# x brought by feature and by token, q's products ahead of v's, and eight expert pieces issued from ScalarE's queue, in a hybrid attention and mixture-of-experts block

## The chip, the core and the metric

The kernel runs on one core of a Trainium2 chip. The metric is the device time of one execution in microseconds (us); lower is better. TensorE (PE) multiplies, VectorE (DVE) and ScalarE (ACT) do elementwise work, GpSimd (POOL) does small work and some transfers, and SyncE (SP) issues most transfers. The DMA engines move data between the chip's memory (HBM) and the core's (SBUF). PSUM takes TensorE's results.

## What is computed

One layer over 512 tokens of 1024 features, all in float32:

```python
h = rmsnorm(x, norm_mix_g)
cb, cc, cu, q, k, v, f_logit, g_conv, g_att = split_cols(h @ w_in)
y_conv = (cb * causal_dwconv3(cc * cu)) @ w_conv_out
o = forgetting_attention(q, k, v, f_logit, b_forget)   # 16 heads of 64
m = sigmoid(g_conv) * y_conv + sigmoid(g_att) * (o @ w_att_out)
x = x + m @ w_out
x = x + hier_moe(rmsnorm(x, norm_ffn_g), ...)          # 32 experts, top 2 of the top group
return rmsnorm(x, norm_final_g)
```

The attention adds to each score the sum of `log_sigmoid(f_logit + b_forget)` between the key's token and the query's.

## The kernel before

**Precision.** An operand of most products is split into a high part (`hi`, a copy on ACT) and a low part (`lo`, a subtraction on DVE), and three products are summed: hi with hi, hi with lo, lo with hi (`mm3`). The expert weights are used as they come, without a split.

**Front (first 62 us).** `hT` holds the normalised x with features on the partitions, in eight blocks `k` of 128 features, hi and lo. Before, x comes by token in four blocks `xs[tb]` of 128 tokens and 1024 features. For each block ACT sums the squares (`square`), DVE makes the root by shifts and three refinement steps (`rsqrt_steps`), DVE, POOL or ACT scale the block by its factor and by `gmix`, PE transposes it eight times (`transp_x`), and ACT and DVE split the result into `hT` (`split_x`). Products for v (`v_mm`, 256 features of v and 16 forget logits) start as soon as a token block is in `hT`. After v come q's two pairs of heads and k's two (`qk_mm`, each 24 products of 512 columns). The forget logits `fz` go through `Abs`, `Exp` and a series on DVE to `acc`; PE transposes `acc` into `pf` between k's first and second pair; DVE scans `pf` and the sums `ncum` go out to HBM (`ncd`) and come back spread over the partitions (`nct`), one row for each head. The front stands in `tc.manual_schedule()`: on each engine its instructions keep the order in which they are written. Instructions from outside such a section (splits for the next heads' weights, transfers) may stand between them.

**Middle.** Attention over 16 heads (to about 240 us) is interleaved with the projections of the other heads. Then come the merges with `w_att_out` and `w_conv_out`, and the short convolution. The planner that orders these parts puts an instruction in its engine's queue where its operands are due; a queue is then worked off in order.

**The w_out stage.** `x2_block(c, tb)` computes 128 tokens by 256 features of `m @ w_out` in 24 products (`px`), DVE adds x, ACT takes the sum of squares. Two PSUM buffers take `px`. The first eight blocks are c = 0 and 1 over the four token blocks; each is followed by `x2_transp`, two transposes on PE and a copy on ACT. The router's weights `wr` come in five small transfers from POOL's queue, and DVE scales them by `gcol` (L727). The stage's last blocks and the routing stand in a hand-ordered section.

**Experts.** 192 pieces of 1 MB (`raw_g`, `raw_u`, `raw_d`) go through a ring of 18 buffers: eight in `wrawb`, which lies where `hT` and the operands of the merges were, two in `wraw` and five in `whl` (which hold `w_out`'s columns until the w_out stage is through with them), and three in `wrawx`. `prefetch(n)` issues the next n pieces on SP's queue. Every expert takes two pieces each of gate, up and down.

Of the kernel before, what the change touches and what calls it, by code (L numbers as in the profile page):

```python
# [24 lines left out]
P = 128  # L25
T = 512
# [18 lines left out]
def block_kernel(ctx, tc, x, norm_mix_g, w_in, w_v0f, conv_w, conv_b, b_forget, w_conv_out,  # L45
# [194 lines left out]
    NV = 4 * NK  # L240
    cols = const.tile([P, NV], F32, name="cols")
    ncd = dram.tile([NH, T], F32, name="ncd")
    with tc.tile_pool(name="s0", bufs=2) as s0:
        xs = [s0.tile([P, D], F32, name=f"xt{tb}", bufs=1) for tb in range(NTB)]
        gmix = s0.tile([P, D], F32, name="gmix", bufs=1)
        vrow = s0.tile([NV, P], F32, name="vrow", bufs=1)
        bfb = s0.tile([P, NH], F32, name="bfb", bufs=1)
        fz = s0.tile([P, NTB, NH], F32, name="fz", bufs=1)
        VW = CW + NH
        with tc.manual_schedule():  # L250
            nc.sync.dma_start(xs[0], x[0:P])
            nc.scalar.dma_start(gmix, norm_mix_g.rearrange("(o d) -> o d", o=1).to_broadcast([P, D]))

            sq0 = s0.tile([P, 1], F32, name="sq0", bufs=1)
            nc.scalar.activation(sq0, eps_t, AF.Square)
            raws, vw = [], ([], [])
            for i in range(2):
                raw = p_tile(f"raw_v{i}")[:, 0:HK * VW].rearrange("p (k f) -> p k f", k=HK)
                nc.sync.dma_start(raw, w_v0f[i].rearrange("p (k f) -> p k f", k=HK))
                raws.append(raw)  # L260
                if i == 0:
                    nc.sync.dma_start(xs[1], x[P:2 * P])
                for r, a in zip(vw, ("hi", "lo")):
                    r.append(pt_tile(a, i)[:, 0:HK * VW].rearrange("p (k f) -> p k f", k=HK))
            for tb in range(2, NTB):
                nc.sync.dma_start(xs[tb], x[tb * P:(tb + 1) * P])
            raws0 = {nm: load_raw(w_cols(c0), nm + "0") for nm, c0 in (("q", COL_Q), ("k", COL_K))}
            nc.scalar.dma_start(bfb, b_forget.rearrange("(o h) -> o h", o=1).to_broadcast([P, NH]))
            for i in range(3):
                nc.gpsimd.dma_start(vrow[i * NK:(i + 1) * NK], conv_w[i].rearrange("(k p) -> k p", p=P))  # L270
            nc.gpsimd.dma_start(vrow[3 * NK:4 * NK], conv_b.rearrange("(k p) -> k p", p=P))
            v_tiles(0)
            ss = [s0.tile([P, 1], F32, name=f"ss{tb}", bufs=1) for tb in range(NTB)]
            rstd = [s0.tile([P, 1], F32, name=f"rstd{tb}", bufs=1) for tb in range(NTB)]
            psv = {}

            def square(tb):
                sq = s0.tile([P, D], F32, tag="sq", name="sq", bufs=1)
                nc.scalar.activation(sq, xs[tb], AF.Square, accum_out=ss[tb])

            def factors(*tbs):
                return rsqrt_steps([(rstd[tb], ss[tb]) for tb in tbs], s0)

            pts = {}

            def scale_x(tb, h):
                hs = slice(h * T, (h + 1) * T)
                nc.vector.scalar_tensor_tensor(xs[tb][:, hs], xs[tb][:, hs], rstd[tb], gmix[:, hs],
                                               op0=ALU.mult, op1=ALU.mult)

            def transp_x(tb):
                for k4 in range(2):
                    pt = ps_t.tile([P, 4, P], F32, tag="t", name="pt")
                    for k in range(4):
                        kk = 4 * k4 + k
                        nc.tensor.transpose(pt[:, k], xs[tb][:, kk * P:(kk + 1) * P], identf)
                    pts[k4] = pt

            def split_x(tb, k4):
                ks, ts_ = slice(4 * k4, 4 * k4 + 4), slice(tb * P, (tb + 1) * P)  # L300
                nc.scalar.activation(hT[0][:, ks, ts_], pts[k4], AF.Copy)
                nc.vector.tensor_sub(hT[1][:, ks, ts_], pts[k4], hT[0][:, ks, ts_].bitcast(F32))

            def lo_v(i):
                for eng, ks in ((nc.vector, slice(0, 2)), (nc.gpsimd, slice(2, 4))):
                    eng.tensor_sub(vw[1][i][:, ks], raws[i][:, ks], vw[0][i][:, ks].bitcast(F32))

            def v_mm(tb, i):
                if i == 0:
                    psv[tb] = (psp if tb % 2 else ps_o).tile([P, 1, VW], F32, tag="proj" if tb % 2 else "o",  # L310
                                                             name=f"psv{tb}")
                for a, b in ((0, 0), (1, 0), (0, 1)):
                    for k in range(i * HK, (i + 1) * HK):
                        nc.tensor.matmul(psv[tb][:, 0], blk(hT[a], k, slice(tb * P, (tb + 1) * P)),
                                         blk(vw[b], k, slice(0, VW)),
                                         start=k == 0 and a == b, stop=k == NK - 1 and b == 1)

            def v_end(tb):
                v_out(0, tb, psv[tb])
                nc.vector.tensor_add(fz[:, tb], psv[tb][:, 0, CW:VW], bfb)  # L320
# [1143 lines left out]
```

## Time and profile before

| | |
|---|---|
| median of 3 runs | 1089.59 us (1088.72 to 1091.97) |
| the profiled execution's own time | 1089.54 us |
| its span, first to last instruction | 1087.9 us |
| mean granted TensorE clock | 0.989 of full speed |
| busy: PE, DVE, ACT, POOL | 97%, 55%, 34%, 4% of the span |
| data moved | 266.17 MB, mean 245 GB/s |
| share of the chain that ended last | PE 84%, DMA 10%, DVE 2%, ACT 2% |

The busy share of PE is no measure of how well it is used, since its matmuls are pipelined. What counts for a stage is which engine or transfer the others wait for there. All times in the text count from the first instruction of the span.

### The profile page before, as it was taken

Reading aid. Unit: us, or ns where it says so; the run is one execution under the profiler, and the core shown is the slowest. Engines: PE = TensorE matmul, PEld = TensorE weight load, DVE = VectorE, ACT = ScalarE, POOL = GpSimd, SP = SyncE. Lnnn points to the kernel's source line nnn. Section 1 sums busy time; section 2 is a strip of 40 time slices with the busy share of each in tenths; the row PEclk is TensorE's granted clock in tenths of the full one; section 3 lists DMA queues with packets and bytes.
Section 4 is the critical chain, followed back from the end, with each engine's and each line's share of the span. In section 5 each row is a group of like instructions: output and inputs, shape, how many; then the busy total and the mean of one; then the engine's idle time right before and its main releaser. Section 6 shows DMA issues by size and latency. Waiting matters only on the chain.

```text
span 1087.9 us, 13684 instructions
## 1 busy us (share of the span) xinstructions
PE 1050.1 (97%) x5281; PEld 680.6 (63%) x5281; DVE 596.2 (55%) x1197; ACT 367.5 (34%) x692; POOL 43.0 (4%) x54
## 2 busy tenths in 40 slices
PE   6999999999999999999989999999999999999993
PEld 4878787878888888888889533333333333433441
DVE  6687878674324444444433545555555555455555
ACT  3576767583223232233332222222222211122114
POOL 4000000000000000000100100000000000000001
PEclk8999999999999999999999999999999999999997
DMA  5321322213232323234495999999999999999992
GB/s 215 117 87 61 99 73 92 95 42 116 80 114 81 114 81 113 78 101 134 171 361 198 376 406 422 419 419 422 419 422 418 421 422 419 420 420 422 422 403 91
DMA packets 41893, 266.17 MB, mean 245 GB/s; under 512 B 5935, under 2 KB 5983, under 8 KB 11745
## 3 DMA queue, kind: packets, MB, share of 16 engines
q1 hardware_dynamic: 35712, 253.05, 58.6%
q10 hardware_dynamic: 3456, 7.61, 2.1%
q0 software_dynamic: 2656, 4.61, 1.2%
q8 instruction: 42, 0.69, 0.3%
q14 instruction: 27, 0.21, 0.1%
HBM read 265.01 MB, written 4.23 MB: 247 GB/s over the span
## 4 chain that ended last, share of the span: by engine, by line
PE 84%; DMA 10%; DVE 2%; ACT 2%; issue 1%; DVEq 0%; ACTq 0%; SPq 0%
PE pg L1069 17%; PE py L124 8%; PE py L1084 8%; PE pg L124 7%; DMA raw_u<-in_w_e_dram 6%; PE pk L1111 5%; PE px L124 4%; PE pu L124 4%; PE pc L124 4%; PE pb L124 4%; DMA raw_d<-in_w_e_dram 4%; PE psq L124 4%; PE psk L124 3%; PE psv L124 3%; PE o L520 2%; PE t L504 1%
## 5 line engine op out<-in xcount | busy, mean ns | idle before, releaser
L1069 PE MATMUL pg<-raw_u,XT 128*64 128x512 f32 x512 | 233.4, 598 | 3.6 <-DMA raw_u<-in_w_e_dram 3.6
L1069 PE MATMUL pg<-raw_g,XT 128*64 128x512 f32 x512 | 234.6, 599 | 0.0
L1112 DVE TENSOR_TENSOR m<-pk,m 128x512 f32<-128x512 f32 x240 | 149.0, 683 | 114.1 <-PE pk L1111 114.1
L1069 PEld LDWEIGHTS pg<-raw_g,XT 128*64 128x64 f32 x512 | 64.3, 136 | 94.4 <-issue 90.9
L1084 PE MATMUL py<-raw_d,hTe 128*64 128x512 f32 x512 | 116.9, 598 | 0.5 <-ACT hTe L1076 0.5
L1257 ACT ACTIVATE ta<-pg,rsl 64x512 f32<-64x512 f32 x32 | 21.9, 683 | 235.7 <-PE pg L1069 235.7
L1069 PEld LDWEIGHTS pg<-raw_u,XT 128*64 128x64 f32 x512 | 64.8, 136 | 32.9 <-issue 15.6
L1094 DVE TENSOR_TENSOR Y<-py,Y 64x512 fp32r<-64x512 f32 x62 | 42.7, 688 | 76.1 <-ACT Y L1093 76.1
L1093 ACT ACTIVATE Y<-py 64x512 fp32r<-64x512 f32 x62 | 36.6, 591 | 121.9 <-PE py L1084 98.7
L1084 PEld LDWEIGHTS py<-raw_d,hTe 128*64 128x64 f32 x512 | 34.0, 136 | 67.1 <-issue 59.7
L1111 PEld LDWEIGHTS pk<-Y,S 128*128 128x128 f32 x240 | 40.4, 188 | 53.8 <-issue 32.5
L1111 PE MATMUL pk<-Y,S 128*128 128x512 f32 x240 | 72.0, 422 | 0.0
L124 PE MATMUL pg<-hT_hi,whl_g 128*128 128x512 f32 x224 | 71.1, 390 | 0.0
L124 PE MATMUL px<-whl_o,mT_hi 128*128 128x256 f32 x256 | 48.4, 290 | 0.0
L124 PEld LDWEIGHTS pg<-hT_hi,whl_g 128*128 128x128 f32 x224 | 41.8, 188 | 8.4
L124 PE MATMUL psq<-hT_hi,whl_q 128*128 128x512 f32 x128 | 44.0, 404 | 0.0
L124 PE MATMUL pg<-hT_lo,whl_g 128*128 128x512 f32 x112 | 43.6, 389 | 0.0
L124 PE MATMUL psk<-hT_hi,whl_k 128*128 128x512 f32 x128 | 42.0, 398 | 0.0
L124 PE MATMUL py<-tT_hi,whl_y 128*128 128x512 f32 x128 | 40.7, 389 | 0.0
L124 PEld LDWEIGHTS px<-whl_o,mT_hi 128*128 128x128 f32 x256 | 40.2, 194 | 0.1
L124 PE MATMUL pb<-hT_hi,whl_b 128*128 128x512 f32 x128 | 40.0, 389 | 0.0
L124 PE MATMUL pc<-hT_hi,whl_c 128*128 128x512 f32 x128 | 40.0, 389 | 0.0
(291 smaller groups left out, 1908.8 us busy)
## 6 DMA issues: line engine op xcount, KB each, us to landing
raw_g<-in_w_e_dram SPq DMA_DIRECT2D x64, 1024.0 KB, 19.9
raw_u<-in_w_e_dram SPq DMA_DIRECT2D x64, 1024.0 KB, 20.4
raw_d<-in_w_e_dram SPq DMA_DIRECT2D x64, 1024.0 KB, 19.9
raw_g<-in_w_in_dram SPq DMA_DIRECT2D x7, 1024.0 KB, 4.8
raw_q<-in_w_in_dram SPq DMA_DIRECT2D x4, 1024.0 KB, 5.7
raw_k<-in_w_in_dram SPq DMA_DIRECT2D x4, 1024.0 KB, 6.6
nct<-ncd ACTq DMA_DIRECT2D x16, 256.0 KB, 3.1
raw_y<-in_w_att_out_dram SPq DMA_DIRECT2D x4, 1024.0 KB, 4.7
```

The costliest lines, as they stand in the source:

```text
L124: nc.tensor.matmul(ps, blk(lhs[a], k, lsl), blk(rhs[b], k, rsl), start=i == 0, stop=i == 3 * NK - 1)
L504: nc.tensor.transpose(ps[:, (qb - kb) * P:(qb - kb + 1) * P], Pt[:, P_OFF[qb] + kb * P:P_OFF[qb] + (kb + 1) * P], identf)
L520: nc.tensor.matmul(po[:, q0:], w, PT[b][:, PT_OFF[kb]:PT_OFF[kb] + n], start=kb == 0 and b == 0, stop=kb == NTB - 1 and b == 1)
L1069: nc.tensor.matmul(ps[r:r + DH], XT[:, k, j], w[k // 4][:, k % 4], start=k == 0, stop=k == NK - 1)
L1084: nc.tensor.matmul(py[n * DH:(n + 1) * DH], hTt[:, f], raws[f // 2][:, f % 2, n * T:(n + 1) * T], start=f == 0, stop=f == 3)
L1093: nc.scalar.activation(Y[hi, ns], py[hi], AF.Copy)
L1094: nc.vector.tensor_sub(Y[lo, ns], py[hi], Y[hi, ns].bitcast(F32))
L1111: nc.tensor.matmul(ps, S[:, tb * P:(tb + 1) * P], Y[:, ns], start=True, stop=True)
L1112: nc.vector.tensor_add(x2[:, tb, ns], ps, x2[:, tb, ns])
L1257: nc.scalar.activation(a, pg[0:DH], AF.Silu, scale=rsl[:, e:e + 1])
```

## The change

x arrives twice. By token (`xs`, two buffers for four blocks) it serves for the sums of squares alone: ACT sums blocks 0 and 2, DVE blocks 1 and 3. By feature (`x_t`, a transposed copy packed outside) it arrives as `xt`, in four pieces of 512 KB. All four factors are made at once (`Sqrt` on ACT, one refinement step on DVE). They are spread over the partitions by one float32 product of a matrix of ones with four diagonal blocks; ACT copies the result to `rb`. Then each feature block k is scaled on DVE (by `gmix`, now a column, and `rb`), copied to `hT` hi on ACT and subtracted to `hT` lo on DVE, and q's six products of that block follow it. v's products and k's come after. PE no longer transposes x, nor the convolution's columns `cols`, which come packed. `gmix` is issued from ACT's queue behind the two squares. k's pairs take the PSUM buffers `psp`, which q's took before; before the change they took `ps_o`. In the w_out stage the first eight expert pieces are written one behind each of the first eight blocks, on ACT's queue; before, they were written behind the loads of w_out's last two columns, on SP's queue. The rest of the ring stays on SP.

```diff
-            nc.sync.dma_start(xs[0], x[0:P])
-            nc.scalar.dma_start(gmix, norm_mix_g.rearrange("(o d) -> o d", o=1).to_broadcast([P, D]))
-            sq0 = s0.tile([P, 1], F32, name="sq0", bufs=1)
-            nc.scalar.activation(sq0, eps_t, AF.Square)
+            rawq = wraw.tile([P, NK, CW], F32, tag="wraw", name="raw_q0")
+            for tb in range(2):
+                nc.sync.dma_start(xs[tb], x[tb * P:(tb + 1) * P])
+            nc.sync.dma_start(rawq[:, 0:HK], wqd[:, 0:HK])
+            sq0 = s0.tile([P, 1], F32, name="sq0")
+            nc.scalar.activation(sq0, eps_t, AF.Sqrt)
+            for tb in range(NTB):
+                sq = s0.tile([P, D], BF, tag=f"sq{tb % 2}", name="sq")
+                if tb >= 2:
+                    xs.append(s0.tile([P, D], F32, tag="xs", name=f"xs{tb}", bufs=2))
+                    nc.sync.dma_start(xs[tb], x[tb * P:(tb + 1) * P])
+                if tb % 2 == 0:
+                    nc.scalar.activation(sq, xs[tb], AF.Square, scale=1.0 / 32, accum_out=ss[:, tb:tb + 1])
+                else:
+                    nc.vector.scalar_tensor_tensor(sq, xs[tb], 1.0 / D, xs[tb], op0=ALU.mult, op1=ALU.mult,
+                                                   accum_out=ss[:, tb:tb + 1])
+            for i in range(0, NK, 2):
+                nc.sync.dma_start(xt[:, i:i + 2], xsrc[:, i:i + 2])
+                if i == 2:
+                    nc.sync.dma_start(rawq[:, HK:], wqd[:, HK:])
+            nc.scalar.dma_start(gmix, norm_mix_g)
...
+            warm(ps_s.tile([P, T], F32, tag="s", name="pwarm0"), 30)
+            nc.scalar.activation(rt_, ss, AF.Sqrt, bias=eps_t)
+            nc.vector.tensor_scalar(vh, ss, EPS, -0.5, op0=ALU.add, op1=ALU.mult)
+            nc.vector.reciprocal(y, rt_)
+            nc.vector.tensor_mul(tn, y, y)
+            nc.vector.tensor_mul(tn, tn, vh)
+            nc.vector.scalar_tensor_tensor(rstd, tn, 1.5, y, op0=ALU.add, op1=ALU.mult)
+            for tb in range(NTB):
+                nc.vector.tensor_scalar_mul(dg[:, tb], identf, rstd[:, tb:tb + 1])
+            nc.tensor.matmul(pss, ones, dg.rearrange("p b t -> p (b t)"), start=True, stop=True)
+            split_q(0)
+            nc.scalar.activation(rb, pss, AF.Copy)
+            def feature(k):
+                nc.vector.scalar_tensor_tensor(xt[:, k], xt[:, k], gmix[:, k:k + 1], rb, op0=ALU.mult, op1=ALU.mult)
+                nc.scalar.activation(hT[0][:, k], xt[:, k], AF.Copy)
+            feature(0)
+            for k in range(NK):
+                if k + 1 < NK:
+                    feature(k + 1)
+                if k == 1:
+                    split_q(1)
+                nc.vector.tensor_sub(hT[1][:, k], xt[:, k], hT[0][:, k].bitcast(F32))
                 for a, b in ((0, 0), (1, 0), (0, 1)):
+                    for j in range(2):
+                        nc.tensor.matmul(psq[j], blk(wq[a], k, slice(j * P, (j + 1) * P)), hT[b][:, k],
                                          start=k == 0 and a == b, stop=k == NK - 1 and b == 1)
+            split_v(0)
+            split_v(1)
+            qk_out("q", 0, psq[0])
+            pv = v_mm(0)
+            wk = split_w(rawk, "k0")
+            for tb in range(1, NTB):
+                pn = v_mm(tb)
+                v_end(tb - 1, pv)
+                pv = pn
+                if tb == 1:
+                    qk_out("q", 1, psq[1])
+            v_end(3, pv)
...
             nc.scalar.activation(az, fz, AF.Abs)
             nc.scalar.activation(e, az, AF.Exp, scale=-1.0)
+            pk = qk_mm("k", 0, wk)
...
-        def prefetch(n):
+        def prefetch(n, eng=nc.sync):
...
-                nc.sync.dma_start(loaded[u], src)
+                eng.dma_start(loaded[u], src)
...
                 for tb in range(NTB):
                     block(o, tb)
+                    prefetch(1, nc.scalar)
                     if c > 0 or tb > 0:
                         x2_transp(c if tb > 0 else c - 1, (tb - 1) % NTB)
             o2 = load_o(2)
             o3 = load_o(3)
-            prefetch(NB_B)
```

## Rows read from the trace of the kernel before

**Rows 1.** Busy us by window: PE, PEld, DVE, ACT, POOL; granted clock, DMA share, GB/s.

```profile
580.00:600.00 20.00, 20.00 (x183) 19.43 (x182) 9.84 (x59) 3.97 (x14) 0.58 (x3) 1.00 0.55 205
640.00:660.00 20.00, 20.00 (x96) 8.02 (x96) 11.90 (x19) 4.65 (x8) 1.00 (x1) 1.00 1.01 419
```

**Rows 2.** Chain that ended last, merged, in order of time: start, us, what.

```profile
553.61 4.15 PE px L124 x24
557.98 2.81 PE px L124 x24
...
900.53 22.10 DMA raw_d<-in_w_e_dram
```

**Rows 3.** Issues on SP's queue: start, us, line, transfer.

```profile
537.70 0.42 SPq L704 DMA_DIRECT2D raw_g<-in_w_e_dram  x1
540.83 0.33 SPq L632 DMA_DIRECT2D m<-in_x_dram  x1
...
545.22 0.33 SPq L704 DMA_DIRECT2D raw_u<-in_w_e_dram  x1
...
590.53 0.33 SPq L704 DMA_DIRECT2D raw_u<-in_w_e_dram  x1
```

**Rows 4.** Timeline around 550 us, DVE and PE: start, us, idle before and releaser.

```profile
551.27 1.27 DVE L727 TENSOR_SCALAR wr<-wr,gcol 128x36 f32<-128x36 f32 x8 [5.46 <-DMA wr<-in_w_router_expert_dram]
552.98 0.63 PE L765 MATMUL pt<-identf,m 128*128 128x128 f32 x2 [3.47 <-issue]
```

**Rows 5.** Windows of 2 us: the columns of rows 1.

```profile
10.00:12.00 2.00, 0.66 (x5) 0.45 (x5) 2.00 (x3) 0.60 (x1) 1.76 (x2) 1.00 1.04 425
...
554.00:556.00 2.00, 2.00 (x12) 2.00 (x11) 1.55 (x3) 1.63 (x3) 0.00 (x0) 0.50 1.00 414
```

**Rows 6.** Transfers by line: queue, count, KB each, median us from issue to landing.

```profile
m<-in_x_dram SPq DMA_DIRECT2D x4, 512.0 KB, 3.5
wr<-in_w_router_expert_dram POOLq DMA_DIRECT2D x4, 32.0 KB, 7.4
gcol<-in_norm_ffn_g_dram POOLq DMA_DIRECT2D x1, 4.0 KB, 3.0
```

**Rows 7.** Timeline of the front: ACT, DVE and ACT's queue.

```profile
6.27 1.06 ACT L279 ACTIVATE sq<-xt 128x1024 f32<-128x1024 f32 x1 [3.38 <-DMA xt<-in_x_dram]
21.01 0.75 DVE L288 SCALAR_TENSOR_TENSOR xt<-xt,rstd,gmix 128x512 f32<-128x512 f32 x1
46.50 0.20 DVE L390 TENSOR_SCALAR f_e<-f_e 128x64 f32<-128x64 f32 x1
52.25 0.23 DVE L400 TENSOR_TENSOR f_acc<-f_acc,fz 128x64 f32<-128x64 f32 x1
66.35 0.33 ACTq L470 DMA_DIRECT2D nct<-ncd  x1
```

**Rows 8.** Chain that ended last, the first 65 us: start, us, what.

```profile
32.59 4.50 PE psv L314 x36
...
37.26 11.10 PE psq L124 x48
...
53.80 0.45 PE pf L404 x4
```

**Rows 9.** Groups by line, first 62 us: busy us, mean ns of one, idle before.

```profile
L302 DVE TENSOR_TENSOR hT_lo<-pt,hT_hi 128x512 fp32r<-128x512 f32 x8 | 5.2, 684 | 3.7 <-ACT hT_hi L301 3.6
L84 DVE TENSOR_TENSOR whl_k<-raw_k,whl_k 128x1024 fp32r<-128x1024 f32 x4 | 4.8, 1224 | 1.8 <-ACT whl_k L83 1.8
L301 ACT ACTIVATE hT_hi<-pt 128x512 fp32r<-128x512 f32 x8 | 4.6, 598 | 10.5 <-PE pt L296 10.5
L223 DVE SCALAR_TENSOR_TENSOR q<-psq,q 64x512 fp32r<-64x512 f32 x4 | 2.8, 689 | 1.4 <-ACT q L222 1.3
L189 DVE TENSOR_TENSOR v<-psv,v 128x128 fp32r<-128x128 f32 x8 | 2.3, 288 | 1.8 <-ACT v L188 1.8
L255 ACT ACT_TABLE_LOAD x1 | 1.3, 1283 | 1.4 <-PEq L1450 1.4
```

More of the change, by code (lines that the diff above doesn't have):

```diff
@@ L236, in proj_qk @@
                 yield
-    NV = 4 * NK
-    cols = const.tile([P, NV], F32, name="cols")
+    cols = const.tile([P, 4 * NK], F32, name="cols")
     ncd = dram.tile([NH, T], F32, name="ncd")
[L243 to L248, printed above, removed]
+    with tc.tile_pool(name="s0", bufs=1) as s0:
+        xt = s0.tile([P, NK, T], F32, name="xt")
+        gmix = s0.tile([P, NK], F32, name="gmix")
+        xs = [s0.tile([P, D], F32, tag="xs", name=f"xs{tb}", bufs=2) for tb in range(2)]
+        ones = s0.tile([P, P], F32, name="ones")
+        bfb = s0.tile([P, NH], F32, name="bfb")
+        fz = s0.tile([P, NTB, NH], F32, name="fz")
@@ L281, in factors @@
[L281 to L297, printed above, removed]
@@ new lines, in block_kernel, with split_q @@
+            v_tiles(0)
+            wq = ([], [])
+            for i in range(2):
+                for r, t in zip(wq, half(f"q0_{i}")):
+                    r.append(t.rearrange("p (k f) -> p k f", k=HK))
+            def split_q(i):
+                split(rawq[:, i * HK:(i + 1) * HK], wq[0][i], wq[1][i])
+            warm(ps_s.tile([P, T], F32, tag="s", name="pwarm0"), 30)
+            nc.scalar.activation(rt_, ss, AF.Sqrt, bias=eps_t)
+            nc.vector.tensor_scalar(vh, ss, EPS, -0.5, op0=ALU.add, op1=ALU.mult)
@@ L345, in block_kernel @@
-            f23 = factors(2, 3)
-            for h in range(2):
-                scale_x(1, h)
-                list(islice(f23, 1 + h))
-            v_mm(0, 1)
-            for tb in range(2, NTB):
-                nc.gpsimd.tensor_mul(xs[tb], xs[tb], gmix)
-            transp_x(1)
-            for k4 in range(2):
-                split_x(1, k4)
-                list(islice(f23, 2))
-            for _ in f23:
-                pass
-            nc.scalar.activation(xs[2][:, 0:T], xs[2][:, 0:T], AF.Copy, scale=rstd[2])
@@ new lines, in block_kernel, with v_mm @@
+            split_v(0)
+            split_v(1)
+            qk_out("q", 0, psq[0])
+            def v_mm(tb):
+                ps = (ps_s if tb % 2 else ps_o).tile([P, 1, VW], F32, tag="s" if tb % 2 else "o", name=f"psv{tb}")
+                for i in range(2):
+                    for a, b in ((0, 0), (1, 0), (0, 1)):
+                        for k in range(i * HK, (i + 1) * HK):
+                            nc.tensor.matmul(ps[:, 0], blk(hT[a], k, slice(tb * P, (tb + 1) * P)),
+                                             blk(vw[b], k, slice(0, VW)),
+                                             start=k == 0 and a == b, stop=k == NK - 1 and b == 1)
+                return ps
@@ new lines, in v_end @@
+            def v_end(tb, ps):
+                nc.vector.tensor_add(fz[:, tb], ps[:, 0, CW:VW], bfb)
+                v_out(0, tb, ps)
+            pv = v_mm(0)
[7 more added lines that the diff above has]
+            v_end(3, pv)
+            az, e, e2, sa, s2, acc = (s0.tile([P, NTB, NH], F32, name=f"f_{c}")
+                                      for c in ("az", "e", "e2", "s", "s2", "acc"))
```

121 lines of the change are left out of this document (27 added, 94 removed).

## The prediction, written before the change was run

> **What bounds the kernel now.** I read the windows first, from the end backwards. In the experts' part the DMA engines are busy all the time, at 419 GB/s [rows 1], and where PE has used up its lead the chain of waits is made of transfers: 22.10 us for one down piece [rows 2]. So the end is set by when this stream begins to run without a break, plus the bytes behind that moment. It begins late. Between 580 and 600 us the DMA engines are only 0.55 busy [rows 1]: the first eight pieces have long been issued, from 537.70 to 545.22, and the ring's next buffer that w_out's columns give back lets a piece go at 590.53 [rows 3]. Those buffers come free as PE works through the w_out stage. Hence two things follow. A us that PE gains anywhere before 590 us moves the stream, and so the end, by a us. And loading the first eight pieces earlier is worth nothing by itself: they are in place before the experts start either way, and the ring is full.
>
> Next I read what PE waits for ahead of 590 us. In the middle it is nearly always busy. Two places remain: the front, and one stall in the w_out stage. There DVE waits 5.46 us for the router's weights `wr` and scales them from 551.27 on; the sum of a block of `px` stands behind that in DVE's queue, PE has no third PSUM buffer, and it idles 3.47 us until 552.98 [rows 4]. Then the granted clock is 0.50, that is 1.2 GHz [rows 5], and the next 24 products take 4.15 us where the following 24 take 2.81 [rows 2]: 1.3 us more. The stall costs 4.8 us. Why is `wr` late? Its transfers are small (32 KB each) and take 7.4 us from issue to landing, while a small load at a quiet time took 3.0 [rows 6]; in these 4 us SP put seven pieces of 1 MB into the queues [rows 3].
>
> **The change, part by part: the pieces on ACT's queue.** Each piece is now written behind a block. ACT works its queue in order, and a block's square waits for DVE, so pieces behind squares leave one per block, about 3 us apart. Against this the planner may place pieces early. It does so on ACT: the sums `nct` for a later head go out at 66.35, before the scores of the heads ahead of it are through [rows 7]. On SP only one piece was placed ahead of the x load (537.70 against 540.83) although all eight lay in freed memory, and seven in a bunch behind it [rows 3]. I take ACT's pieces as spread, not one per block, so that two to four MB lie ahead of `wr` where eight did. The landing of `wr` then lies between 3.0 and 7.4 us [rows 6]. I take 5.9, 1.5 earlier than before. PE's stall shrinks from 3.47 to about 2.0. After idle stretches of that kind the clock stood at 1.00 (PE busy 0.66 of 2 us, [rows 5]), so I count the 1.3 us of slow products as saved too. The pieces cost ACT some 0.4 us each to issue [rows 3], eight times 3.2 us; ACT waits for most of this stage, but one issue can stand ahead of the last split of `mT` that PE needs: 0.3. Sum: -1.5 - 1.3 + 0.3 = **-2.5**. Bounds: -4.8 (no stall left) and +1.3 (a bunch as before, with `wr` a little later). The other pieces stay on SP; nothing there is moved past them but the last x load, which is now free of seven pieces behind it.
>
> **The front.** The anchor is `pf`, which ends at 53.80 + 0.45 = 54.25 [rows 8]: k's second pair and `nct` follow it in both kernels at the same distance. I build the new front up to there.
>
> - *Sums of squares.* A block of x took until 6.27 with `gmix` of the same size beside it [rows 7]; alone I take 5.0 for block 0 and 6.2 for block 1. ACT's square takes 1.06 [rows 7] and its sum 0.2; block 2 can only be issued then, at 6.3, and needs 3.5 [rows 6]: 9.8. DVE's square of block 1 is twice an instruction of 0.75 [rows 7]: 7.7, block 3 lands at 11.2, its square ends at 12.7.
> - *Factors.* Root on ACT, five tiny DVE steps of about 0.2 and four diagonal blocks (a 128x128 step took 0.29, [rows 9]): 15.1. The float32 product of 512 columns is not in the front; between one product of this width (0.23, 11.10/48, [rows 8]) and four of them, doubled by the clock (1.8), I take 0.6. ACT's copy 0.60 [rows 9]: 16.3.
> - *Eight feature blocks.* DVE does 0.75 [rows 7] and 0.68 [rows 9], with hops 1.5, so 12.0, and once 1.22 for the second half of q's low weights [rows 9]: 29.5. PE needs 11.1 for q's 48 products [rows 8] and runs behind DVE, even if its first products run at the lower clock. Two products are left after the last subtraction: 29.9.
> - *v and k.* 96 products of v at 4.50/36: 12.0; k's first pair 11.10/2 = 5.5 [rows 8]. PE is through at 47.4.
> - *Forget sums.* From 29.5 DVE has v's two low halves (about 1.3 each, from 1.22), q's four outputs at 0.69, k's two low halves at 1.22, v's eight outputs at 0.29 [rows 9]: 10.1, and many of them take turns with ACT. v's last block ends on PE at 41.9; I take its logits at 43.8. `Abs` and `Exp` are 0.3 each. `Exp` comes after `Sqrt` now, and a table load of 1.28 [rows 9] stands before it; before the change the front had one load, at 1.4 us, off the path. 45.7. The series ran from 46.50 to 52.48 with two splits of 1.22 inside [rows 7, 9]: 3.5 by itself, 45.7 + 3.5 = 49.2, and about half a split between: 49.8. PE waits for it from 47.4. `pf` ends at 50.3.
>
> So the front is worth 54.25 - 50.3 = **-4.0**. The transposes that PE no longer does and the refinement steps are all in this sum, since it was built afresh. Bounds: -6.4, if the sums come early and `pf` follows at 47.4; and -0.5, if `gmix`, issued behind ACT's second square at about 11, takes 7.4 as `wr` did among big loads (18.4 where 16.3 is needed), and the series a whole split more with the turns in full.
>
> The Trainium skill has a rule for the table load ("ScalarE: Activation LUTs", section "Table sets: the hidden batching unit"): exp and sqrt lie in different sets, and a switch costs about 2.66 us, since a drain of some 1.38 comes with the load. The trace has 1.28 for the load and shows no drain by itself. By the page `pf` would come 1.4 later, and the sum would be 1084.4.
>
> **Sum**, against the profiled execution's 1089.54 us (span 1087.9; the median of the runs is 1089.59): 1089.54 - 4.0 - 2.5 = 1083.0.
>
> **Rivals.**
>
> - *The pieces leave in a bunch.* For it: [rows 7], and seven in a bunch on SP. Then PE's stall stays: 1089.5 - 4.0 + 0.3 = 1085.8, 1084.5 to 1087.5.
> - *The front is lost.* `gmix` late by 2.1, the series late; PE idles between k's first pair and `pf` for five us or more, longer than the 3.47 that were followed by the lower clock [rows 4, 5], and pays 1.3 more. Front -0.5 + 1.3, stage -2.5 or 0: 1087.8 to 1090.3.
> - *Slower: a third queue starves `wr`.* With the eight pieces bunched on ACT, the x load on SP and `wr` on POOL, three queues share the engines. 8.4 MB at 419 GB/s [rows 1] are 20 us; if `wr` lands only when the pieces are through, at about 560 instead of 551.27, PE stalls 8.8 longer: 1089.5 - 4.0 + 8.8 = 1094. It decides from a landing at 558.5, which eats the front's 4.0 and 3.3 more. Against it: beside eight pieces on SP, `wr` landed after 7.4 [rows 6], long before they were through. The Trainium skill ("DMA: Bandwidth & Descriptors", section "Queues, rings and completion order") says that each engine takes turns among its queues by packet; by that a third queue takes a share from `wr` only while the x load lasts, about 1.3 us, and the time would be that of the bunch, near 1087.
>
> **Chances.** Forecast 0.50, bunch 0.28, front lost 0.14, slower 0.08. A measurement of this kernel tells a difference of about 0.3%, 3.3 us, from no change. Faster by more (below 1086.3): 0.46 of the forecast, 0.15 of the bunch, 0.03 of the third: 0.64. Slower by more (above 1092.8): 0.08, and 0.02 of the third: 0.10. Same: 0.26. Range: the two likeliest cases reach from 1078.3 (both bounds) to 1087.5, the third to 1090.3. I give 1078.5 to 1089.5, which leaves out most of the slower case and a part of the third. The likeliest one's own range is 1079 to 1086.
>
> **What would show it.** Right, if `pf` ends at about 50 us, q's products begin near 17 and DVE sets their pace, DVE's wait for `wr` is nearer to 4 us than to 5.5, no window after it shows the lower clock, and the piece now at 590.53 goes out some 6 us earlier, with the rest unchanged. Wrong, if the pieces follow each other on ACT's queue within 4 us, if `gmix` ends DVE's wait before the first feature block, or if PE idles longer than 4 us ahead of `pf`; and altogether if the end does not move with the piece of 590.53.

## The result, and the profile after

| | before | after |
|---|---|---|
| median, runs side by side | 1089.15 us (4 runs) | 1100.30 us (4 runs, 1098.80 to 1101.89) |
| the profiled execution, its span | 1089.54, 1087.9 | 1098.80, 1097.1 |
| mean granted TensorE clock | 0.989 | 0.983 |

The change is slower: the ratio is 1.0101, with a 95% interval of 1.0080 to 1.0122, so 11 us, where 6.5 us less were forecast. The end did move with the stream: the piece that went out at 590.53 [rows 3] goes out at 599.59 now, 9.06 later, and the span is 9.2 longer. So the loss lies ahead of that point. The attention's read-out begins 3.2 us later (257.8 against 254.6, the first of the 128 `py` products of `oT_hi`), and the w_out stage adds another 5.9.

Timeline of the front after the change, rows of SP, DVE, PE and ACT: start, us, engine, line, instruction, idle time before it and what ended it.

```profile
6.06 1.62 SPq L265 DMA_DIRECT2D xs<-in_x_dram  x2
...
12.95 1.22 DVE L269 SCALAR_TENSOR_TENSOR sq<-xs 128x1024 bf16<-128x1024 f32 x1 [5.48 <-DMA xs<-in_x_dram]
...
19.08 1.41 DVE L320 SCALAR_TENSOR_TENSOR xt<-xt,gmix,dg 128x512 f32<-128x512 f32 x2 [1.67 <-ACT dg L315]
...
23.52 1.22 DVE L84 TENSOR_TENSOR whl_q<-raw_q,whl_q 128x1024 fp32r<-128x1024 f32 x1 [1.64 <-ACT whl_q L83]
...
30.99 1.47 DVE L329 TENSOR_TENSOR hT_lo<-xt,hT_hi 128x512 fp32r<-128x512 f32 x2
...
16.34 2.08 PE L313 MATMUL pss<-dg,ones 128*128 128x512 f32 x2 [6.81 <-DVE dg L312]
20.55 2.07 PE L332 MATMUL psq<-hT_hi,whl_q 128*128 128x512 f32 x4 [2.13 <-ACT hT_hi L321]
...
25.41 0.73 PE L332 MATMUL psq<-hT_lo,whl_q 128*128 128x512 f32 x2 [0.23 <-DVE hT_lo L329]
...
34.16 0.67 PE L348 MATMUL psv<-PThi,hT_hi 128*128 128x272 f32 x4
...
55.94 1.01 PE L385 MATMUL pf<-identf,f_acc 128*16 128x128 f32 x4 [4.07 <-DVE f_acc L382]
...
50.23 0.25 ACT L369 ACTIVATE f_az<-fz 128x64 f32<-128x64 f32 x1
50.50 1.28 ACT L370 ACT_TABLE_LOAD   x1
51.79 0.26 ACT L370 ACTIVATE f_e<-f_az 128x64 f32<-128x64 f32 x1
```

The last block of x lands at 12.95, the float32 product that spreads the factors takes 2.08 after 6.81 us of idle, and the first feature block starts at 19.08. At 25.41 PE waits for the low half of the second block. That subtraction stood in DVE's queue behind the second half of q's low weights (23.52), for which DVE had waited 1.64 for ACT's copy. PE then still has 38 of q's 48 products to do, 8.75 us up to v's first product at 34.16, while DVE is through with its last subtraction at 32.46. `Abs` stands at 50.23, 4.0 us behind v's last product. PE then waits 4.07 us for the series, and `pf` ends at 56.95 where it ended at 54.25 [rows 8]. What follows is slow as well. The chain that ended last, first of the kernel after, then of the same front with the old ring (start, us, what):

```profile
55.94 1.01 PE pf L385 x4
56.95 6.59 PE psk L124 x24
```

```profile
56.06 1.01 PE pf L385 x4
57.07 7.85 PE psk L124 x24
```

24 such products take half of 11.10, 5.55 [rows 8]; here 6.59 and 7.85. The windows of the kernel after (columns as in [rows 1]) show the lower clock at the start and behind the idle stretch:

```profile
0.00:20.00 20.00, 10.37 (x32) 3.73 (x32) 6.63 (x20) 5.76 (x10) 3.43 (x12) 0.87 0.82 283
20.00:40.00 20.00, 19.23 (x95) 16.21 (x96) 16.83 (x22) 12.42 (x17) 0.00 (x0) 0.87 0.36 142
...
50.00:60.00 10.00, 5.93 (x23) 4.38 (x22) 5.41 (x18) 3.53 (x7) 1.35 (x3) 0.83 0.02 5
...
550.00:560.00 10.00, 7.87 (x59) 7.70 (x58) 1.93 (x10) 1.56 (x6) 0.00 (x0) 0.88 0.77 237
...
570.00:580.00 10.00, 7.38 (x46) 6.74 (x46) 5.48 (x6) 5.17 (x9) 0.00 (x0) 0.83 0.84 310
```

The w_out stage after the change, same view, rows of ACT and its queue, DVE and PE:

```profile
540.91 0.34 ACTq L684 DMA_DIRECT2D raw_g<-in_w_e_dram  x1
542.37 0.34 ACTq L684 DMA_DIRECT2D raw_u<-in_w_e_dram  x1
549.26 0.33 ACTq L684 DMA_DIRECT2D raw_g<-in_w_e_dram  x1
...
571.66 0.34 ACTq L684 DMA_DIRECT2D raw_u<-in_w_e_dram  x1
572.32 3.89 ACT L83 ACTIVATE whl_o<-raw_o 128x1024 fp32r<-128x1024 f32 x4
...
547.81 0.17 DVE L726 TENSOR_SCALAR vs<-vi 128x4 int32<-128x4 int32 x1 [4.09 <-POOL vi L724]
...
555.50 1.28 DVE L707 TENSOR_SCALAR wr<-wr,gcol 128x36 f32<-128x36 f32 x8 [6.44 <-DMA wr<-in_w_router_expert_dram]
...
548.78 0.44 PE L745 MATMUL pt<-identf,m 128*128 128x128 f32 x2 [2.31 <-DVE m L738]
557.20 0.41 PE L745 MATMUL pt<-identf,m 128*128 128x128 f32 x2 [2.13 <-issue]
571.66 0.41 PE L745 MATMUL pt<-identf,m 128*128 128x128 f32 x2 [0.39 <-DVE m L738]
573.42 0.39 PE L124 MATMUL px<-whl_o,mT_hi 128*128 128x256 f32 x1 [1.35 <-ACT whl_o L83]
574.68 0.58 PE L124 MATMUL px<-whl_o,mT_hi 128*128 128x256 f32 x1 [0.87 <-DVE whl_o L84]
```

The pieces do leave spread out, 540.91 to 571.66, two of them ahead of x's load. But there are two stalls of PE ahead of 560 instead of one of 3.47 [rows 4], and a third place at 571 to 575 that did not exist (0.39, 1.35 and 0.87): the four splits of w_out's last two columns, on ACT and then on DVE, stand behind all eight pieces. Before, DVE had them at 538.98, 554.45, 555.93 and 566.58, between the blocks. DVE's small steps on the tokens' numbers (`vs`) moved as well: before, they stood behind the first sum of `px`; now they are ahead of it, and wait 4.09 for POOL. PE's waits in the stage add up to 7.05 us, against 3.47; that is 3.6 of the 5.9. The products between them are slower as well: the granted clock is 0.83 from 570 to 580.

### The profile page after: what moved, and what is told of

It is laid out like the page before. It is cut to its first block, busy times and chain, and to the rows that moved or that the text cites. A ratio compares the mean times of both kernels' runs of the same rounds, so it can differ in the third digit from the quotient of the medians.

```text
span 1097.1 us, 13606 instructions
## 1 busy us (share of the span) xinstructions
PE 1051.5 (96%) x5260; PEld 681.0 (62%) x5260; DVE 593.5 (54%) x1173; ACT 366.0 (33%) x689; POOL 33.1 (3%) x48
## 4 chain that ended last, share of the span: by engine, by line
PE 74%; DMA 18%; DVE 4%; ACT 2%; issue 1%; POOL 0%; SPq 0%; DVEq 0%; ACTq 0%
PE pg L1050 13%; DMA raw_u<-in_w_e_dram 11%; PE py L124 8%; PE pg L124 7%; PE py L1065 6%; DMA raw_d<-in_w_e_dram 5%; PE pu L124 4%; PE pc L124 4%; PE pb L124 4%; PE px L124 4%; PE pk L1092 4%; PE psk L124 3%; PE psv L124 3%; PE psq L124 3%; PE o L500 2%; PE t L484 1%
## 5 line engine op out<-in xcount | busy, mean ns | idle before, releaser
L124 PE MATMUL pu<-hT_hi,whl_u 128*128 128x512 f32 x128 | 40.0, 389 | 0.0
```

The lines of the kernel that those rows point to most:

```text
L124: nc.tensor.matmul(ps, blk(lhs[a], k, lsl), blk(rhs[b], k, rsl), start=i == 0, stop=i == 3 * NK - 1)
```

## The experiments

Ratios are to the kernel before, timed beside each; the medians of before were 1089.05 to 1089.50. Where the intervals of two runs overlap, the difference between them is not shown.

| run | median us | ratio, 95% interval |
|---|---|---|
| e1 front alone | 1094.77 | 1.0047 (1.0031 to 1.0062) |
| e2 ring alone | 1094.62 | 1.0049 (1.0036 to 1.0062) |
| e3 ring in its new places, SP's queue | 1093.90 | 1.0040 (1.0027 to 1.0054) |
| e4 before without DVE's two waits | 1084.47 | 0.9953 (0.9940 to 0.9966) |
| e8 e4 and ring on ACT's queue | 1089.53 | 1.0001 (0.9993 to 1.0010) |
| e9 ring on POOL's queue behind wr | 1087.72 | 0.9984 (0.9975 to 0.9993) |
| e12 e8, splits early | 1091.78 | 1.0017 (1.0006 to 1.0028) |
| e13 e12, first four pieces on SP | 1084.47 | 0.9957 (0.9943 to 0.9971) |
| e5 e1, 62 warm products | 1094.63 | 1.0048 (1.0034 to 1.0062) |
| e6 e1, `pf` behind k's second pair | 1094.04 | 1.0042 (1.0029 to 1.0055) |
| e7 e1, Exp's table early | 1092.73 | 1.0033 (1.0023 to 1.0043) |
| e10 e1, forget chain early | 1089.28 | 0.9997 (0.9988 to 1.0006) |
| e14 e10, four blocks of x at once | 1085.82 | 0.9966 (0.9955 to 0.9976) |
| e11 e10 and e4's stage | 1084.23 | 0.9953 (0.9940 to 0.9967) |
| e15 e14 and e4's stage | 1082.47 | 0.9938 (0.9925 to 0.9951) |

### The two halves of the change

**e1**, the front with the old ring:

```diff
-                    prefetch(1, nc.scalar)
...
             o3 = load_o(3)
+            prefetch(NB_B)
```

> The changed kernel with the ring as it was: the eight pieces again behind the loads of w_out's columns on SP's queue. My theory says that the two halves of the change add: the front costs +3.3 us (the read-out products py start at 257.99 in the changed kernel, 254.72 before), the w_out stage +5.8. So this kernel should be 3.3 us slower than the one before, near 1092.5, with the w_out stage (start of py 254.7 +3.3; wr's wait 5.5, PE's stall 3.5; four splits of o2 and o3 between 553 and 567 less their shift) as before. The rival, that the front is good for its predicted -4.0 once the ring does not disturb it, expects 1085.1; a third, that the front's own late end is hidden further on, expects 1089.2.

5.3 us slower. The stage is as before (one stall of 3.65). The front is dearer than the 3.2 us read off the kernel after, because the 24 products behind `pf` took 7.85 here and 6.59 there; up to that point the two executions differ by 0.1 us.

**e2**, the ring's edit in the kernel before:

> The kernel before with nothing but the ring's edit: one piece behind each of the first eight blocks, on ACT's queue. My theory: the stage costs +5.8 us by itself, so about 1095, with three things in the trace: DVE waits about 4 us for POOL's iota ahead of the first sums of px, PE stalls about 2 us for them, and the four splits of o2 and o3 stand behind all eight pieces at about 569, with PE waiting for them. The rival says that this order is a result of the new front (a different start of the stage in the plan) and that the ring alone gives the predicted -2.5, near 1087.

5.2 us slower, with the stalls of the kernel after (2.28, 1.27, 0.39, 1.35 and 0.88). The halves add: 5.3 + 5.2 = 10.5 of 11.

**e3**, the changed kernel with `prefetch(1)` where it has `prefetch(1, nc.scalar)`:

> The changed kernel with the pieces written in the same places, behind the blocks, but issued from SP's queue. If what costs 5.8 us is that the pieces are work of ACT in the plan, which then moves the splits behind them and the steps on the tokens' numbers ahead of the sums, this kernel has the order of before on ACT and DVE and is near 1092.5, like the one with the front alone. If what costs is the place (pieces issued later, in turn with the blocks) or the load on the DMA engines, it stays near 1098 to 1100.

4.4 us slower, the same as the front alone within the intervals; one stall of 3.73, the splits between the blocks. So the place in the program costs nothing; the queue, with what follows from it, does.

### What the stage's price is made of

**e4**, `gcol` into ACT's copies of the transposed x2, and POOL's `iota` moved ahead of the `wr` transfers:

```diff
-            for k in range(NK):
-                nc.vector.tensor_scalar_mul(wr[:, k, 0:36], wr[:, k, 0:36], gcol[:, k:k + 1])
...
-                nc.scalar.activation(x2T[c][:, :, tb * P:(tb + 1) * P], pt, AF.Copy)
+                for k in range(2):
+                    nc.scalar.activation(x2T[c][:, k, tb * P:(tb + 1) * P], pt[:, k], AF.Copy,
+                                         scale=gcol[:, 2 * c + k:2 * c + k + 1])
```

> The kernel before, with DVE's wait for the router's weights taken away: gcol multiplies the transposed x2 where ACT copies it, not wr, and POOL makes the tokens' numbers ahead of the wr transfers. This asks for the price that my prediction put on the stall alone: 3.5 us of PE idle and 1.3 of slow products, so -4.8, near 1084.7, with the piece that goes out at 590.53 leaving at about 585.7. The rival: PE's stall is only moved (to the splits of w_out's last columns, or to ACT, which gets 16 more short copies), and the time stays within 1 us of before.

5.0 us faster; PE has no stall in the stage, and the ring's piece leaves at 585.30, where 585.7 was expected (issue on SP's queue: start, us, line, transfer):

```profile
585.30 0.33 SPq L704 DMA_DIRECT2D raw_u<-in_w_e_dram  x1
```

So the price that the prediction put on the stall, 4.8, was right.

**e9**, `prefetch(NB_B, nc.gpsimd)` in the kernel before: the pieces on POOL's queue, seven of eight behind `wr`.

> The kernel before, with the eight pieces on POOL's queue, seven of them behind the five transfers of the router's weights wr, so that only one piece and w_out's columns are ahead of or beside wr; ACT's and DVE's orders stay, but for the small steps on the tokens' numbers. My prediction held that the pieces make wr late (7.4 us from issue to landing): by it wr lands after 3 to 5 us here, DVE's wait falls from 5.5 to 2 or 3 us, and the time falls by 2 to 4.8, to 1084.5 to 1087. The rival, which the runs so far speak for (7.2 to 8.7 us whether the pieces are bunched or spread), says that wr is slow by itself, since it is made of packets of 16 and 32 bytes: it lands after about 7, the stall stays at 3.5, and the time at 1089.

Transfers by line (queue, count, KB each, median us from issue to landing), DVE's wait in e9 and PE's stall there:

```profile
wr<-in_w_router_expert_dram POOLq DMA_DIRECT2D x4, 32.0 KB, 6.8
```

```profile
549.64 1.28 DVE L727 TENSOR_SCALAR wr<-wr,gcol 128x36 f32<-128x36 f32 x8 [4.87 <-DMA wr<-in_w_router_expert_dram]
...
551.35 0.41 PE L765 MATMUL pt<-identf,m 128*128 128x128 f32 x2 [2.23 <-issue]
```

6.8 us with one piece ahead, 7.4 with eight beside it [rows 6], as medians of four transfers. What DVE waits for is the last of them. That wait ends at 549.64 and not at 551.27, 1.6 earlier (1.2 if counted from the first issue of `wr`), and PE's stall is 2.23 and not 3.47. So the pieces account for 1.2 to 1.6 us of `wr`'s lateness, and the rest is its own. The time falls by 1.8.

**e8**, e4 with the ring on ACT's queue:

> The kernel before with the ring's edit and without DVE's two waits (gcol taken into ACT's copies of the transposed x2, POOL's tokens' numbers ahead of the wr transfers), to be set beside the same kernel with the old ring, which took 1084.5. What is left of the ring's price is then what the late splits of o2 and o3 cost. My theory says about 4 us, 1088.5: the four splits still stand behind the eight pieces and PE waits for them at about 569. The rival: the price was the two waits, and this kernel takes 1084 to 1085.

5.1 us above e4. The four splits stood behind the pieces, and PE waited 1.59 and 0.88 for them, as expected; a wait of 0.39 just ahead was for the last sum. That this is the whole price was put to the test in **e12**: the loads of the last two columns written earlier.

```diff
                     block(o, tb)
+                    if c == 0 and tb == 2:
+                        o2 = load_o(2)
+                    if c == 1 and tb == 2:
+                        o3 = load_o(3)
                     prefetch(1, nc.scalar)
...
-            o2 = load_o(2)
-            o3 = load_o(3)
```

> The kernel before with the ring on ACT's queue and without DVE's two waits, as in the run that took 1089.5, and with the loads of w_out's last two columns written earlier, behind the third block of each of the first two columns, so that their splits stand between the pieces and not behind all eight. If the late splits are the rest of the ring's price, the time falls by about 5 us to that of the same kernel with the old ring, 1084.5, and PE no longer waits at 565. The rival: the pieces themselves cost it (issues among ACT's squares and copies, a third queue), and the time stays at 1088.5 to 1089.5.

My theory fell: the splits stood between the blocks, and the time did not fall; it rose by 2.3 in the medians (1.7 by the ratios, whose intervals touch). The timeline of e12, DVE and PE, names another wait:

```profile
553.65 0.42 DVE L756 TENSOR_TENSOR m<-px,m 128x256 f32<-128x256 f32 x1 [5.98 <-DMA m<-in_x_dram]
...
554.18 0.66 PE L763 MATMUL pt<-identf,m 128*128 128x128 f32 x2 [3.72 <-DVE m L756]
556.18 0.80 PE L124 MATMUL px<-whl_o,mT_hi 128*128 128x256 f32 x2 [1.34 <-ACT whl_o L83]
```

The fourth block's sum needs x's last load, and that is late. From issue to landing it took 8.0 us before (the row in [rows 6] is the median of four x loads and hides it), 8.2, 7.8 and 8.9 in e1, e3 and e4, and 11.9 and 11.7 in e2 and e8. The transfer rows of e2:

```profile
m<-in_x_dram SPq DMA_DIRECT2D x1, 512.0 KB, 11.9
wr<-in_w_router_expert_dram POOLq DMA_DIRECT2D x4, 32.0 KB, 8.7
```

**e13**, e12 with the first four pieces on SP's queue and the last four on ACT's:

```diff
-                    prefetch(1, nc.scalar)
+                    prefetch(1, nc.scalar if c > 0 else nc.sync)
```

> The last kernel (ring behind the blocks, no waits of DVE, splits of w_out's last columns early, 1091.8), with the first four pieces on SP's queue, behind which x's last load stands as before, and only the last four on ACT's. Theory: what costs now is x's last load. It shares the DMA engines with pieces on ACT's queue, lands 11.7 to 12 us after its issue where it took 8.0 to 8.9 in kernels without pieces there, and the sum of the fourth block waits for it (5.98 us in the last kernel, PE 3.7). So here x lands after 8 to 9, that wait is gone, and the time is that of the old ring without DVE's waits, 1084.5 (to 1085.5). Rival: pieces issued from ACT cost by themselves, or the order of the splits does: 1088 or more.

1084.47, the time of e4 to the hundredth, with four pieces still issued from ACT; PE has no stall, and x lands after 7.9 (that the medians agree to the hundredth is chance; within the intervals they are the same):

```profile
m<-in_x_dram SPq DMA_DIRECT2D x1, 512.0 KB, 7.9
```

In e8 the same late x cost PE 0.59 only, and the splits 2.47 with a clock of 0.86 around them; in e12 it is the other way round. In e2, and in the kernel after, the late x cost nothing, since DVE was still waiting for `wr` when x had landed (552.25 and 552.74 in e2). Which wait counts depends on the order; both come with the first pieces on ACT's queue. So neither ACT's issues nor pieces behind squares were seen to cost anything. What costs is the first pieces on ACT's queue, and what they reorder. e13 also gave ACT and DVE nearly the order of before, so it does not part x's load from the order by itself; that the load matters with the splits in place is e12's row.

Why x is late is not settled. In the kernel after, e2, e8 and e12 two pieces, 2 MB, go out ahead of x's load (in e2 at 537.51 and 538.97, x at 540.35). In all other runs one does (before: 537.70, x at 540.83). At the 415 GB/s of the kernel before, 1 MB more takes 2.5 us, by estimate, and x is 2.8 to 3.9 later. e9 speaks for this second reading: its pieces were on POOL's queue beside SP's, one ahead of x, and x landed after 8.7. Two pieces on SP's own queue ahead of x would decide it, and were not tried. The same doubt holds for `wr`, which is late too in these runs, 8.4 to 9.1 against 6.8 to 7.5 in the others.

### The front

**e5**, 62 warm products instead of 30:

> The front alone (changed kernel, ring as before), with 62 warm products at the start where there were 30, so that PE is busy until the float32 product that spreads the factors. In the front alone PE idled 6.8 us ahead of that product, which took 2.08 us and was followed by a clock of 0.86 over the first 40 us. My theory puts about 1 us of the front's loss on that product and 1 to 2 on q's first products at the lower clock: pf ends 1 to 2.5 us earlier than its 57.1 there, time about 1092.5 against 1094.8. Rival: DVE sets the pace of the eight feature blocks, PE catches up in any case, and only the product's own us is won or nothing.

Nothing (1094.63 against e1's 1094.77). The float32 product took 1.12 instead of 2.08, and DVE's first block began at 18.29, 0.9 earlier than in e1. But PE idled 2.14 and 2.28 between q's products, and those behind the second idle were slow, four in 1.70 where four take 1.07 later on. PE in e5:

```profile
24.63 0.72 PE L332 MATMUL psq<-hT_lo,whl_q 128*128 128x512 f32 x2 [2.28 <-DVE hT_lo L329]
25.19 1.70 PE L332 MATMUL psq<-hT_hi,whl_q 128*128 128x512 f32 x4
...
34.99 0.67 PE L348 MATMUL psv<-PThi,hT_hi 128*128 128x272 f32 x4
```

v's first product came at 34.99, later than the 34.26 of e1, and `pf` at 56.77, not 56.06; only the 24 products behind `pf` were quicker, 6.33 against 7.85. So PE waits for DVE up to the second block's low half, and from there on its own products set q's end. That is neither the prediction's reading, in which DVE sets the pace to the end, nor this run's theory.

**e6**, `pf` behind k's second pair:

```diff
             pk = qk_mm("k", 0, wk)
+            pk1 = qk_mm("k", 1, wk)
...
-            qk_out("k", 1, qk_mm("k", 1, wk))
+            qk_out("k", 1, pk1)
```

> The front alone, with pf's four transposes written behind k's second pair, so that PE does not wait for the forget series between the pairs. My theory: the 4.1 us of idle ahead of pf and the slow products behind it (5 to 11 of them, 1 to 2.5 us) are the price of the late series; without them k's second pair ends near 57.4, against 64.8, and the time falls by 5 to 6 us to about 1089. Rival: the sums nct come some 1.5 us later by this and the first scores have to wait for them, so that most of it is lost again: 1092 to 1094.

0.7 us won, not 5, and even that lies within the intervals. PE's idle is gone and comes back behind it: 2.57 and 0.97 for k's outputs, which now stand behind the scan, and the first use of `nct` waits until 65.70. The rival was right about the loss; it is shared between k's outputs and `nct`.

**e7**, one `Exp` of a single column on ACT behind v's splits:

> The front alone, with one Exp of a single column on ACT ahead of q's outputs, so that the table of Exp is loaded there (ACT has time then) and not between Abs and Exp. The load of 1.28 us leaves the forget chain: pf earlier by 1.3, and by up to 2.7 if the Trainium skill's figure for a switch (page ScalarE: Activation LUTs, section Table sets: the hidden batching unit) holds with its drain of 1.38. Time about 1093.5 against 1094.8, or 1092 with the drain and with fewer slow products behind a shorter idle. Rival: the load at its new place delays q's outputs and with them v's, and nothing is won.

2.0 us below e1 in the medians, 1.5 by the ratios, whose intervals overlap: a gain is not shown. The load is off the chain (`Abs` 51.44, `Exp` 51.72), but `Abs` is 1 us later, `pf` begins only 0.2 earlier (55.86 against 56.06), and PE still idles 3.30.

**e10**, that and the order of the forget chain:

```diff
-            def v_end(tb, ps):
+            def f_end(tb, ps):
                 nc.vector.tensor_add(fz[:, tb], ps[:, 0, CW:VW], bfb)
-                v_out(0, tb, ps)
...
+                f_end(tb - 1, pv[tb - 1])
+                if tb < 3:
+                    v_out(0, tb - 1, pv[tb - 1])
...
             nc.vector.tensor_add(acc, acc, fz)
+            for tb in (2, 3):
+                v_out(0, tb, pv[tb])
```

> The front alone (changed kernel, ring as before) with the forget chain taken out of the queue behind v's outputs: the logits of the last two token blocks are added first, Abs, Exp and the series follow, the outputs of v's last two blocks come behind the series, and Exp's table is loaded early. My theory is that pf is late because of these queues (v's last product ended at 46.2, Abs stood at 50.2, the load took 1.28): now Abs stands near 47.3, the series ends near 51.5, pf near 52 right behind k's first pair with no idle of PE and no slow products behind it, the sums nct come near 60 and py starts near 252.4, 2.2 us earlier than before the change: about 1087, 8 us below the front alone. Rival: the front is late by its beginning (factors, feature blocks), and no order behind it brings pf below 54: 1089 to 1091.

5.5 us below e1, level with before; `pf` begins at 53.05, py at 253.9, not 252.4. Timeline of ACT and PE:

```profile
48.61 0.26 ACT L370 ACTIVATE f_az<-fz 128x64 f32<-128x64 f32 x1 [0.52 <-DVE fz L355]
48.90 0.26 ACT L371 ACTIVATE f_e<-f_az 128x64 f32<-128x64 f32 x1
...
53.05 0.60 PE L388 MATMUL pf<-identf,f_acc 128*16 128x128 f32 x4 [1.25 <-DVE f_acc L383]
```

This idle of 1.25 is not followed by slow products: `pf` takes 0.60, not 1.01. `Abs` is 1.3 later than I expected, since a split for the next heads still stands ahead of it.

**e14**, e10 with room for all four token blocks (the third and fourth in v's raw buffers) and 46 warm products:

```diff
-        xs = [s0.tile([P, D], F32, tag="xs", name=f"xs{tb}", bufs=2) for tb in range(2)]
+        xs = [s0.tile([P, D], F32, tag="xs", name=f"xs{tb}", bufs=2) if tb < 2 else p_tile(f"xs{tb}")[:, 0:D]
+              for tb in range(NTB)]
```

> The front with the early forget chain (1089.3), with buffers for all four token blocks of x, so that the third and fourth are loaded at once and not behind the squares of the first two, and 46 warm products. My prediction had the factors spread (rb) at 16.3; they came at 19.0, with the fourth block landing at 12.9 and the float32 product 2.08 us at the lower clock. Theory: the fourth block lands near 8.6, the factors are 4 us earlier, q, v and k follow, and pf ends near 49.5: py near 250.2, time about 1085.5. Rival: x by feature now comes behind the four blocks and DVE's and PE's pace from there to v's end stays, with later transfers of q's and v's weights in the way: less than 2 us won.

3.5 us below e10, 3.6 below before. The timeline, DVE and PE:

```profile
10.18 1.22 DVE L267 SCALAR_TENSOR_TENSOR sq<-xs 128x1024 bf16<-128x1024 f32 x1 [2.85 <-DMA xs<-in_x_dram]
...
13.57 1.13 PE L311 MATMUL pss<-dg,ones 128*128 128x512 f32 x2 [0.69 <-DVE dg L310]
...
50.71 0.60 PE L386 MATMUL pf<-identf,f_acc 128*16 128x128 f32 x4 [1.06 <-DVE f_acc L381]
```

The fourth block lands at 10.18 instead of 12.95, and `pf` begins at 50.71: nearly the 49.85 of the prediction.

**e11** and **e15**, the fronts of e10 and e14 with the stage of e4:

> The front with the early forget chain and the w_out stage without DVE's two waits, ring as before. If the two add: 1084.5 (stage alone) less 2.2, near 1082.3. If the stage gives back what the front gains or the stream does not follow, 1084 to 1085.

> The same front, and the w_out stage without DVE's two waits (old ring). If the front's gain reaches the end beside the stage's: 1084.4 less 4, near 1080.5. If not: 1083 to 1084.5, as with the front of the run before.

e11 is no faster than e4, as its front is level with before. e15 takes 1082.47, 6.9 us below before and 17.8 below the change as it was made; of the two gains (5.0 in e4 and 3.6 in e14, together 8.6) it keeps four fifths in the medians. In its profiled execution the ring's piece goes out at 581.54, 9.0 earlier than before. Against e4 alone its 2.0 us lie within the intervals; in the profiled executions the piece goes out 3.8 earlier than in e4. Where the rest goes behind that was not tried.

## Why the prediction was wrong

The anchor held: before 590 us each us of PE is a us of the end. Both terms of the sum had the wrong sign, -4.0 where +5.3 came (e1), and -2.5 where +5.2 came (e2).

**The stage.** Three steps failed.
- "I take 5.9, 1.5 earlier than before" for `wr`. It landed after 8.4, later than the 7.4 of before. The 1.5 was about right for what the pieces cost `wr` (1.2 to 1.6 in e9), but there seven of the eight stood behind it and one ahead. In the kernel after two went out ahead, the least of the "two to four MB" that I allowed, and the third only at 549.26; yet `wr` came later. How much of that is the second piece ahead, and how much the other queue, was not tried. The rest of `wr`'s time is its own: the premise that large pieces hold it up was read off two rows of unlike transfers [rows 6]; `gcol` is one transfer, `wr` five on a queue that takes 0.9 us to issue each.
- "The last x load, which is now free of seven pieces behind it." Pieces behind it on its own queue did it no harm; two pieces ahead of it on another queue did (11.9 in e2), though in the kernel after this was hidden behind `wr` and counts only once that wait is gone (e12). It is the mechanism of my slower rival, at another transfer: x, not `wr`. The Trainium skill's rule ("DMA: Bandwidth & Descriptors", section "Queues, rings and completion order"), that an engine takes turns among its queues, would fit the 8.0 and 11.9, but no run here shows it: one piece more ahead of x fits them as well, and in e9 pieces on POOL's queue beside x left it at 8.7. I had used the rule for `wr` and not asked it of x.
- What the pieces push aside. I counted their issues (0.3 us) and not that the planner now orders ACT and DVE anew around eight more instructions of ACT: the splits of w_out's last columns behind them, the `vs` steps ahead of the sums. In e2 PE waited 2.28 for the first sums, and 1.35 and 0.88 for the splits, with slow products around them. e3 shows that the queue is the cause, for with the same places on SP's queue the order is that of before. How the planner weighs an issue was not tried.

What was right: the pieces are paced, if not one by one from the start, and the stall's price of 4.8 (5.0 in e4).

**The front.** By the prediction's steps, forecast and trace: the fourth block lands 11.2, 12.95; the float32 product 0.6, 2.08; first feature block 16.3, 19.08; q's end (v's first product) 29.9, 34.16; v 12.0, 12.1; k's first pair 5.5, 5.5; from v's end to `Exp`'s end 3.8, 5.8; series 3.5 and half a split, 3.7 and none. So v's and k's products were sized well. Four things failed:
- The start was 2.8 late. The fourth block's load took 5.5 us from its issue, not 3.5, and the float32 product took 2.08, not 0.6; without an idle stretch ahead it still takes 1.12 (e5).
- q lost another 1.5. The sum said that PE "runs behind DVE, even if its first products run at the lower clock", and so let DVE's stretch of 13.2 set q's end, with 0.4 from the last subtraction to v's first product. DVE's stretch came out at 13.4, but by luck, since two errors cancel: 1.27 a block and not 1.5, and 1.64 of waiting for ACT's copy of q's weights. What set the end was PE, which had 38 of 48 products left when the second block's low half came at 25.41; from DVE's last subtraction to v's first product it needed 1.7. The slow products of q ahead of 25.41 cost nothing, since PE waited there all the same.
- The chain from v's logits to `Exp` was 2.0 too short. I had counted DVE's work there at 10.1 us, but not three splits for the next heads (1.22 each) that the planner set in between, nor that `Abs` stands in ACT's queue behind v's last outputs.
- The lower clock behind 4.07 us of idle is the case of the rival "the front is lost", which I gave 0.14 and priced at 1.3 for the clock; it cost 1.0 to 2.3. The sign that I had named for it, PE idle for more than 4 us ahead of `pf`, came.

e10 and e14 give the two parts back, 5.5 and 3.5, and with both the front is worth 3.6. That this is near the 4.0 of the sum is partly luck: e14 has four buffers, 46 warm products and another order, which the sum did not have. What the runs show is that the order of the forget chain and the late fourth block made the front lose.

For the table load the trace decides against the Trainium skill's figure ("ScalarE: Activation LUTs", section "What ACT_TABLE_LOAD costs"), by which a drain of about 1.38 us comes with a load of about 1.28: `Abs` ends at 50.48, the load runs from 50.50 to 51.78, and `Exp` starts at 51.79. The load's own 1.28 agrees; no drain stands beside it.

## What to carry to other kernels

A transfer moved to another engine's queue is to be priced at three places: what it now goes out ahead of or beside (here x's last load), what its issuing engine does around it, and what a planner reorders because of it; the last is read from the order of instructions, not from durations. When a chain of small steps ends at a product that PE waits for, count what stands ahead of each step in its engine's queue, also what other parts of the program may put there. And a wait is best removed by taking its operand off the path (e4) before hoping that the transfer gets faster.

## What the hardware showed that I had not expected

- Two kernels with the same instructions up to that point (the kernel after and e1), after nearly the same idle of PE (4.07 and 4.09 us), had 24 products take 6.59 in one execution and 7.85 in the other, with granted clocks of 0.83 and 0.76 between 50 and 60 us. At the start it is alike: behind an idle of 2.28 four products of q took 1.70 (e5, clock 0.83 from 20 to 30), and behind one of 2.26 in e15 the clock stayed at 1.00.
- The DMA engines can be as busy and move less. In the kernel before, the 10 us with `wr`'s transfers and the next 10 differ by a quarter in GB/s at nearly the same busy share (windows, columns as in [rows 1]); that the small transfers are the cause is inferred, and was not tried alone:

```profile
540.00:550.00 10.00, 9.51 (x80) 9.13 (x78) 2.45 (x13) 1.79 (x6) 4.50 (x7) 1.00 1.03 311
550.00:560.00 10.00, 7.02 (x47) 7.05 (x48) 4.72 (x13) 4.00 (x10) 0.00 (x0) 0.83 1.00 415
```

- A 512 KB load took 3.5 us as the median of four [rows 6] and 8.0 for the last of the four. In the kernel before even that cost nothing, since DVE waited longer for `wr`; in e12 it decides, and there it took longer still. The median hid it.
